# Moving the start of TensorE's SBUF tiles to multiples of 128 bytes in a hybrid decoder layer

## The chip, the cores and the metric

The kernel runs on one core of one Trainium2 chip. The metric is the device time of one execution in microseconds; each run gives one such time, and the median of three runs stands for the kernel.

## What is computed

One decoder layer on x of shape (1, 1024, 1024), float32. The reference, cut to its frame:

```python
def hybrid_layer(x, ...):
    h = rms_norm(x, norm1_g)
    z = h @ w_in                                  # 1024 x 2304
    ...                                           # pool | short conv | conformer conv | differential attention
    mix = jnp.concatenate([y_pool, y_sconv, y_conf, y_attn], axis=-1)
    x = x + mix @ w_out                           # 1024 x 1024
    h2 = rms_norm(x, norm2_g)
    x = x + (jax.nn.silu(h2 @ w_gate) * (h2 @ w_up)) @ w_down   # 1024 x 2816, 2816 x 1024
    return x
```

## The kernel before, in words

**The products.** Every large product is made to nearly full float32 precision of three matmuls in the type float32r: each operand is split into a rounded part (hi) and the rest (lo), and `mm3` (L133) adds hi·hi, hi·lo and lo·hi in PSUM. The first argument of a matmul is the stationary operand (`lhsT`, 128 columns, loaded before it), the second the moving one (`rhs`, up to 512 columns, streamed through). `mms` (L579) is the same three as a generator, so that they can be put between other work.

**The weights.** `wsplit` (L120) brings 128x1024 of a weight by DMA into a staging tile `st` (pool `stp`), casts it into `whi` (ACT, L116) and takes the rest into `wlo` (POOL, L130). Those two lie in pool `wp`, or in tiles of the tags `dw`, `pt0` and `pt1` in other pools.

**The stages.** They follow one another on TensorE, with overlap at the seams:

- Input projections into channels (`chunk_mm`, L222): the moving operand is `hT` (the normalized, transposed x, four tiles `hT00` to `hT11`), the stationary one `whi` or `wlo`. First with 256 columns (192 matmuls) while x is normalized, then with 512 (480). Beside them VectorE makes the convolutions (`conv_taps`, L292, its steps at L300) and GpSimd the pooling sums (`winsum`, L382).
- Projections of k, q and v (`proj_tok`, L449): the weight moves (256 columns), `hT` is stationary (576 matmuls).
- Attention in 16 units (`unit`, L633), between whose steps the output projection is put (`gen_partial`, L584, and `out_attn`, L718; its matmuls stand at L580 to L582, the weight moves with 512 columns, the tiles `sp`, `mh`, `ml` are stationary). `gen_partial` has 288 of them, `out_attn` 96.
- Gate and up (`gu_mm`, L785, and `gu_items`, L821): `h2` (tiles `h2a`, `h2b`, `h2c`, `h2lo`, `h2hi`) moves with 512 columns, the weight is stationary. There are 22 column tiles, 2 matrices, 2 halves of the sequence, 8 contraction tiles and 3 products: 2112 matmuls, into the PSUM tiles `pg` and `pu`.
- Down (`down`, L884): the weight moves with 512 columns, the activation tiles `a` are stationary; 11 groups of 96, 1056 matmuls into `pd`. In the first ten groups the weight is in the tag `dw`, in the last in `wp`.

The scheduler that orders each engine's work is the tile framework's (`schedule_with_timeline_sim`), with `tc.issue_after` at some places.

**Where a tile lies.** SBUF is 128 partitions of bytes; a tile begins at one byte address in all of them. Pools with `side="left"` are laid from low addresses upward behind a descriptor scratch of 16,384 bytes, pools with `side="right"` from the top (229,344) downward; a tile's size is rounded up to 32 bytes. Pool `sm` (small tiles) takes 5,056 bytes, 39.5 times 128, so that everything on the left behind it begins 64 bytes past a multiple of 128. The top is 96 bytes past one, and so is every large tile on the right. In the built program the operands of the large projections begin so many bytes past a multiple of 128:

| matmuls | columns | moving operand | stationary operand |
|---|---|---|---|
| projections into channels | 256, 512 | `hT`: 96 | `wp`: 0 |
| k, q, v | 256 | `wp`: 0 | `hT`: 96 |
| output projection | 512 | `wp`: 0 | `sp`, `mh`, `ml`: 64 |
| gate, up: 1968 | 512 | `h2`: 64 | `wp`: 0 |
| gate, up: 144, at the seam to attention | 512 | `h2`: 64 | `pt0`, `pt1`: 96 |
| down, first ten groups (960) | 512 | `dw`: 64 | `a`: 64 |
| down, last group (96) | 512 | `wp`: 0 | `a`: 64 |

A slice within a tile begins a multiple of 512 bytes further on, so that its offset is its tile's. In the text below such a pair is written (moving, stationary), (64, 0) for gate and up.

Of the kernel before, what the change touches and what calls it, by code (L numbers as in the profile page):

```python
# [11 lines left out]
F = mybir.dt.float32  # L12
# [7 lines left out]
P = 128  # L20
# [46 lines left out]
def tile_hybrid(ctx, tc, x, norm1_g, w_in, pool_w, pool_scale, sconv_w, conf_w, conf_b, ln_g, ln_b,  # L67
                q_g, k_g, lq1, lk1, lq2, lk2, subln_g, w_out, norm2_g, w_gate, w_up, w_down,
                rel_bias, onehot, maskrow, cntinv, out):
    nc = tc.nc  # L70
    V, A, G, T = nc.vector, nc.scalar, nc.gpsimd, nc.tensor
# [11 lines left out]
    def pool(name, bufs=1, side="left", **kw):  # L83
        return tc.tile_pool(name=name, bufs=bufs, side=side, reuse_waits="tile", **kw)
# [2 lines left out]
    stp = ctx.enter_context(pool("stp", 2))  # L87
    wp = ctx.enter_context(pool("wp", 6))
    sm = ctx.enter_context(pool("sm"))
    dram = ctx.enter_context(tc.tile_pool(name="dram", bufs=1, space=DRAM))  # L90
    m8 = ctx.enter_context(pool("m8", 3))
    spp = ctx.enter_context(pool("spp", 4))
# [12 lines left out]
    make_identity(nc, ident)  # L105
    mhalf = const.tile([P, 16], F, name="mhalf")
    G.memset(mhalf, -0.5)

    def col(name, src, n, pl=const):
        t = pl.tile([P, n], F, name=name)  # L110
        dma(out=t, in_=src.rearrange("o (c p) -> p (o c)", p=P))
        return t
# [846 lines left out]
```

## Time and profile before

| | |
|---|---|
| runs | 1191.39, 1189.75, 1190.41 us |
| median | 1190.41 us |
| the profiled execution: span from the first to the last instruction | 1189.3 us |
| TensorE matmul busy | 1143.7 us (96%) |
| VectorE, GpSimd, ScalarE busy | 570.3, 388.2, 338.6 us |
| bytes moved by DMA | 62.50 MB, 53 GB/s on the mean |

The profile gives no time of the profiled execution beyond its span; the median of the runs is 1.1 us longer than this span, which is the start and the end of the program. A matmul's duration in the profile (0.39 us for 512 columns) overlaps with its neighbours; what a matmul costs in a stream is the distance from its start to the next one's, and that is read from the timeline as the first and the last start of a stream and the number of matmuls between them.

### The profile page before, as it was taken

What the parts mean: (1) busy time and instruction counts of PE and PEld (TensorE: products, weight loads), DVE (VectorE), ACT (ScalarE), POOL (GpSimd) and SP (SyncE); (2) the same over time, 40 slices, a digit from 0 to 9 for tenths busy, and PEclk for the clock granted to TensorE, in tenths of its full rate; (3) what the DMA queues carried; (4) which work ended last, traced back from release to release, by engine and by line L of the source; (5) the groups of instructions that cost most, each with busy time, mean ns of one, the idle gap of its engine ahead of it and who ended that gap; (6) DMA issues with size and microseconds to landing.
All of it is one profiled execution on the core that took longest, in us unless ns stands there. A gap on an engine that the chain in (4) does not pass through costs nothing.

```text
span 1189.3 us, 13724 instructions
## 1 busy us (share of the span) xinstructions
PE 1143.7 (96%) x5563; PEld 944.9 (79%) x5563; DVE 570.3 (48%) x916; ACT 338.6 (28%) x614; POOL 388.2 (33%) x260
## 2 busy tenths in 40 slices
PE   7999399999989999999999999999999999999998
PEld 7877279997778768888888888888888888888887
DVE  5698984648999875314232322414132322314134
ACT  5411012546776765310212112020212112020200
POOL 5239224655677532320312221130312122130300
PEclk8999599999999999999999999999999999999999
DMA  8121111111121110311211111120211111120103
GB/s 214 53 62 36 36 35 37 37 37 36 36 81 36 45 54 19 107 53 36 71 36 54 53 36 54 36 60 30 72 36 53 53 41 49 36 71 19 53 1 141
DMA packets 85678, 62.50 MB, mean 53 GB/s; under 512 B 15560, under 2 KB 76528, under 8 KB 85616
## 3 DMA queue, kind: packets, MB, share of 16 engines
q1 hardware_dynamic: 85616, 61.64, 17.2%
q8 instruction: 43, 0.70, 0.2%
q14 instruction: 19, 0.16, 0.0%
HBM read 57.43 MB, written 4.20 MB: 52 GB/s over the span
## 4 chain that ended last, share of the span: by engine, by line
PE 83%; DVE 8%; issue 3%; ACT 2%; DMA 2%; POOL 1%; SPq 1%; ACTq 0%; POOLq 0%
PE pd L135 7%; PE pd L136 7%; PE pd L134 7%; PE pg L136 7%; PE pu L135 7%; PE pg L134 7%; PE pg L135 7%; PE pu L136 7%; PE pu L134 7%; PE mm L134 4%; PE mm L135 4%; PE mm L136 4%; DVE mixC L300 2%; PE fm L580 1%; PE fm L582 1%
## 5 line engine op out<-in xcount | busy, mean ns | idle before, releaser
L130 POOL TENSOR_TENSOR wlo<-st,whi 128x1024 fp32r<-128x1024 f32 (+1 forms) x92 | 238.3, 2597 | 631.9 <-ACT whi L116 611.4
L116 ACT CAST whi<-st 128x1024 fp32r<-128x1024 f32 x90 | 94.5, 1051 | 461.4 <-PE pd L135 207.3
L795 DVE TENSOR_TENSOR aa<-sg,pu 128x512 f32<-128x512 f32 x44 | 30.3, 688 | 338.6 <-PE pu L136 337.8
L894 DVE TENSOR_TENSOR x<-x,pd 128x512 f32<-128x512 f32 x176 | 120.1, 687 | 135.2 <-PE pd L136 135.1
L136 PE MATMUL pd<-whi,a 128*128 128x512 f32 x352 | 137.3, 390 | 0.0
L135 PE MATMUL pd<-wlo,a 128*128 128x512 f32 x352 | 137.3, 390 | 0.0
L134 PE MATMUL pd<-whi,a 128*128 128x512 f32 x352 | 137.2, 390 | 0.0
L135 PE MATMUL pu<-h2lo,whi 128*128 128x512 f32 x256 | 101.4, 396 | 0.0
L135 PE MATMUL pg<-h2lo,whi 128*128 128x512 f32 x256 | 101.3, 396 | 0.0
L300 DVE SCALAR_TENSOR_TENSOR mixC<-u,cw,mixC 128x1023 f32<-128x1023 f32 (+29 forms) x60 | 91.1, 1548 | 0.8
L135 PE MATMUL mm<-hT,whi 128*128 128x512 f32 (+1 forms) x224 | 82.8, 374 | 1.3 <-DVE hT L196 1.3
L134 PE MATMUL mm<-hT,whi 128*128 128x512 f32 (+1 forms) x224 | 80.9, 376 | 2.8 <-DVE t L428 1.6
L136 PE MATMUL mm<-hT,wlo 128*128 128x512 f32 (+1 forms) x224 | 82.3, 371 | 0.0
L135 PEld LDWEIGHTS pd<-wlo,a 128*128 128x128 f32 x352 | 66.1, 188 | 14.3
L134 PEld LDWEIGHTS pd<-whi,a 128*128 128x128 f32 x352 | 66.2, 188 | 14.0
L136 PEld LDWEIGHTS pd<-whi,a 128*128 128x128 f32 x352 | 66.1, 188 | 13.9
L798 DVE TENSOR_TENSOR a<-aa,a 128x512 fp32r<-128x512 f32 x44 | 63.7, 1447 | 25.2 <-ACT a L797 25.2
L134 PE MATMUL pg<-h2hi,whi 128*128 128x512 f32 x176 | 69.8, 396 | 0.0
L136 PE MATMUL pg<-h2hi,wlo 128*128 128x512 f32 x176 | 69.7, 396 | 0.0
L134 PE MATMUL pu<-h2hi,whi 128*128 128x512 f32 x176 | 69.7, 396 | 0.0
L136 PE MATMUL pu<-h2hi,wlo 128*128 128x512 f32 x176 | 69.7, 396 | 0.0
L797 ACT CAST a<-aa 128x512 fp32r<-128x512 f32 x44 | 27.2, 617 | 110.4 <-DVE aa L795 110.4
(266 smaller groups left out, 2333.9 us busy)
## 6 DMA issues: line engine op xcount, KB each, us to landing
st<-in_w_gate_dram SPq DMA_DIRECT2D x22, 512.0 KB, 3.7
st<-in_w_up_dram SPq DMA_DIRECT2D x22, 512.0 KB, 3.7
st<-in_w_down_dram SPq DMA_DIRECT2D x22, 512.0 KB, 3.4
st<-in_w_in_dram SPq DMA_DIRECT2D x18, 512.0 KB, 3.7
xt<-in_x_dram SPq DMA_DIRECT2D x8, 512.0 KB, 7.8
st<-in_w_out_dram SPq DMA_DIRECT2D x8, 512.0 KB, 3.5
xr<-in_x_dram SPq DMA_DIRECT2D x16, 256.0 KB, 2.6
out_dram<-x SPq DMA_DIRECT2D x7, 512.0 KB, 2.6
```

What stands on the lines that cost most here:

```text
L116: A.copy(dst, src)
L130: G.tensor_tensor(lo[:, nv:], st[:, nv:], hi[:, nv:].bitcast(F), op=ALU.subtract)
L134: T.matmul(ps, lhsT=L[0], rhs=Rr[0], start=first, stop=False)
L135: T.matmul(ps, lhsT=L[0], rhs=Rr[1], start=False, stop=False)
L136: return T.matmul(ps, lhsT=L[1], rhs=Rr[0], start=False, stop=last)
L300: V.scalar_tensor_tensor(acc[:, s:], u[:, :S - s], w[:, j:j + 1], acc[:, s:], op0=ALU.mult, op1=ALU.add)
L580: yield lambda: T.matmul(ps, lhsT=L[0], rhs=Rr[0], start=first, stop=False)
L582: yield lambda: T.matmul(ps, lhsT=L[1], rhs=Rr[0], start=False, stop=last)
L795: V.tensor_tensor(aa, sg, pu, op=ALU.mult)
L797: A.copy(a[0][:, j, sl], aa)
L798: V.tensor_tensor(a[1][:, j, sl], aa, a[0][:, j, sl].bitcast(F), op=ALU.subtract)
L894: V.tensor_tensor(x1[t][:, sl], x1[t][:, sl], ps, op=ALU.add)
```

## The change

Two tiles are added that nothing reads. `padl` (64 bytes) stands at the start of pool `sm`, and `padr` (96 bytes) is the first thing on the right side; each gets a memset on GpSimd. The descriptor scratch is halved to 8,192 bytes, since with both pads the left and the right side would no longer fit beside each other.

```diff
     stp = ctx.enter_context(pool("stp", 2))
     wp = ctx.enter_context(pool("wp", 6))
     sm = ctx.enter_context(pool("sm"))
+    padl = sm.tile([P, 16], F, name="padl")
+    padr = ctx.enter_context(pool("padr", side="right")).tile([P, 24], F, name="padr")
...
     G.memset(mhalf, -0.5)
+    G.memset(padl, 0.0)
+    G.memset(padr, 0.0)
...
-    nc = _bacc.Bacc("TRN2", target_bir_lowering=False, num_devices=1)
+    nc = _bacc.Bacc("TRN2", target_bir_lowering=False, num_devices=1, dynamic_dma_scratch_size=8192)
```

In the built program of the change all operands of the table above begin at a multiple of 128 bytes, every pair is (0, 0). Tiles that TensorE reads in smaller steps move too: `pt`, `KT`, `QT`, `VV`, `kst` to 0, the normalized x before its transposes (`xn`) from 32 to 96, `sa` and `pu` of the pooling part from 32 to 96 (`pu1` from 96 to 32). The staging tiles `st` stay at 0.

The instructions of TensorE, VectorE, ScalarE and SyncE are the same, in the same order. Only GpSimd's differ, at its start, before (the tile `ident` is the identity for transposes, `rn` the first norm of x):

```order
masks.py:197 MEMSET ident 128x128
L107 MEMSET mhalf 128x16
L363 MEMSET anti 128x128
masks.py:199 ISA
masks.py:199 AFFINE_SELECT ident<-ident 128x128
L367 MEMSET bd 128x256
L364 AFFINE_SELECT anti<-anti 128x128
L169 TENSOR_SCALAR rn<-ssf 128x1
```

and with the change (its lines are 2 to 4 further on):

```order
masks.py:197 MEMSET ident 128x128
L109 MEMSET mhalf 128x16
L110 MEMSET padl 128x16
L111 MEMSET padr 128x24
masks.py:199 ISA
masks.py:199 AFFINE_SELECT ident<-ident 128x128
L367 MEMSET anti 128x128
L371 MEMSET bd 128x256
L368 AFFINE_SELECT anti<-anti 128x128
L173 TENSOR_SCALAR rn<-ssf 128x1
```

Two small memsets have come ahead of the making of `ident`, and the memset of `anti` has moved behind it.

## Rows read from the trace of the kernel before

**Rows 1.** The page: busy time by engine, and the chain's shares by engine.
```profile
PE 1143.7 (96%) x5563; PEld 944.9 (79%) x5563; DVE 570.3 (48%) x916; ACT 338.6 (28%) x614; POOL 388.2 (33%) x260
PE 83%; DVE 8%; issue 3%; ACT 2%; DMA 2%; POOL 1%; SPq 1%; ACTq 0%; POOLq 0%
```
**Rows 2.** Busy time by stage: us, each engine's busy us, clock, DMA share, GB/s.
```profile
53.00:141.00 88.00, 68.33 (x275) 51.22 (x274) 83.11 (x66) 13.61 (x18) 51.10 (x20) 0.89 0.19 54
141.00:190.00 49.00, 48.81 (x202) 38.71 (x203) 39.43 (x36) 5.78 (x8) 9.93 (x5) 0.96 0.11 33
190.00:269.00 79.00, 79.00 (x684) 79.00 (x683) 38.95 (x78) 37.15 (x74) 47.28 (x36) 1.00 0.11 34
269.00:440.00 171.00, 158.75 (x876) 130.02 (x876) 148.92 (x375) 119.37 (x273) 102.91 (x102) 0.99 0.16 50
440.00:541.00 101.00, 100.39 (x453) 80.48 (x452) 35.02 (x52) 35.74 (x58) 27.87 (x15) 1.00 0.20 58
541.00:1163.00 622.00, 622.00 (x2693) 506.39 (x2691) 184.91 (x233) 97.52 (x127) 129.42 (x54) 1.00 0.15 44
1163.00:1189.30 26.30, 22.38 (x98) 18.05 (x96) 11.70 (x17) 0.00 (x0) 0.00 (x0) 1.00 0.40 160
```
**Rows 3.** Timeline of TensorE, gate and up, (64, 0): start us, us, instruction.
```profile
1041.24 0.39 PE L134 MATMUL pu<-h2a,whi 128*128 128x512 f32 x1
...
1074.84 0.39 PE L134 MATMUL pd<-whi,a 128*128 128x512 f32 x1
```
**Rows 4.** Timeline of TensorE, down, its tenth group, (64, 64).
```profile
1141.45 0.39 PE L134 MATMUL pd<-whi,a 128*128 128x512 f32 x1
...
1163.00 0.39 PE L136 MATMUL pd<-whi,a 128*128 128x512 f32 x1
```
**Rows 5.** Timeline of TensorE, down, its last group, (0, 64).
```profile
1163.22 0.40 PE L134 MATMUL pd<-whi,a 128*128 128x512 f32 x1
...
1184.98 0.40 PE L136 MATMUL pd<-whi,a 128*128 128x512 f32 x1
```
**Rows 6.** Timeline of TensorE, up with its weight in `pt1` and `pt0`, (64, 96).
```profile
483.36 0.40 PE L135 MATMUL pu<-h2lo,whi 128*128 128x512 f32 x1
...
496.89 0.39 PE L136 MATMUL pu<-h2hi,wlo 128*128 128x512 f32 x1
```
**Rows 7.** Timeline of TensorE, projections into channels, (96, 0).
```profile
160.01 0.39 PE L135 MATMUL mm<-hT,whi 128*128 128x512 f32 x1
...
176.33 0.40 PE L136 MATMUL mm<-hT,wlo 128*128 128x512 f32 x1
```
**Rows 8.** Timeline of TensorE, projections of k, q, v, 256 columns, (0, 96).
```profile
249.62 0.28 PE L136 MATMUL mm<-whi,hT 128*128 128x256 f32 x1
...
257.91 0.28 PE L136 MATMUL mm<-whi,hT 128*128 128x256 f32 x1
```
**Rows 9.** Timeline of TensorE, projections into channels at half clock, (96, 0).
```profile
142.20 0.63 PE L136 MATMUL mm<-hT,wlo 128*128 128x512 f32 x1
...
143.91 0.63 PE L134 MATMUL mm<-hT,whi 128*128 128x512 f32 x1
```
**Rows 10.** Busy time of TensorE in that stretch: us, busy, clock, DMA share, GB/s.
```profile
141.19:144.60 3.41, 3.41 (x8) 0.50 0.00 0
```
**Rows 11.** Groups of TensorE instructions by line and form: busy us, mean ns, idle before.
```profile
L135 PE MATMUL mm<-hT,whi 128*128 128x512 f32 x160 | 64.0, 400 | 0.0
L135 PE MATMUL mm<-wlo,hT 128*128 128x256 f32 x192 | 54.1, 282 | 0.0
```
**Rows 12.** Waits of TensorE: us in total, times, longest us.
```profile
PE mm L417 <- DVE t L428: 15.2, 1, 15.2
```
**Rows 13.** The page's DMA queues: packets, MB, share of the 16 engines.
```profile
q1 hardware_dynamic: 85616, 61.64, 17.2%
```
**Rows 14.** Timeline of GpSimd at the start.
```profile
0.86 0.11 POOL L107 MEMSET mhalf<- 128x16 f32 x1
...
5.38 0.31 POOL L169 TENSOR_SCALAR rn<-ssf 128x1 f32<-128x1 f32 x1 [3.43 <-ACT xn L166]
```

## The prediction

> **What bounds the kernel now.** First the page: TensorE is busy in 96% of the span and makes 83% of the chain that ended last [rows 1]. Then the stages [rows 2]: from 440 us on TensorE is busy in 100.4 of 101, 622 of 622 and 22.4 of 26.3 us, and in 190 to 269 us in all of 79, while VectorE and GpSimd have far less to do there. In those stages what each matmul takes off passes straight to the end. In 269 to 440 us (attention) TensorE has 158.8 us and VectorE 148.9 of 171: the chain alternates. In 53 to 141 us VectorE is busy in 83.1 of 88 us, and TensorE ends that stage in a wait of 15.2 us for it [rows 2, 12]: what TensorE gains before 141 us only lengthens that wait.
>
> Third, the cost of one matmul in a stream, read as the first and the last start and the count between. A clock at full speed should need 512 columns' time and no more. At half clock that is so: four steps take 1.71 us, 427.5 ns each, with the clock at 0.50 [rows 9, 10], one column in each cycle of 1.2 GHz. Half of it, 213.3 ns, is what 2.4 GHz would give. At full clock every stream is slower than that, and by how much goes with where the two operands begin:
>
> - (64, 0), gate and up: 144 matmuls in 33.60 us, 233.3 ns [rows 3]
> - (64, 96), up at the seam: 58 in 13.53 us, 233.3 ns [rows 6]
> - (96, 0), channels: 70 in 16.32 us, 233.1 ns [rows 7]
> - (0, 64), last down group: 95 in 21.76 us, 229.0 ns [rows 5]
> - (64, 64), other down groups: 95 in 21.55 us, 226.8 ns [rows 4]
> - (0, 96), 256 columns: 71 in 8.29 us, 116.8 ns, against 106.7 [rows 8]
>
> So 13 to 20 ns of each matmul, 6 to 9%, are lost at full clock alone, which points to the reading of operands and not to the array. The least is lost where both operands begin at the same offset. No row shows (0, 0) for such a matmul; it has to be bounded.
>
> **The price of (0, 0).** Take the loss over 213.3 ns as a sum: a part b that always stands, A if the moving operand begins off a multiple of 128, B if the stationary one does, C if the two offsets differ. The four kinds of 512 columns give b+A+B = 13.5, b+A+C = 20.0, b+A+B+C = 20.0 and b+B+C = 15.7. Hence C = 6.5, B = 0, A = 4.3 and b = 9.2: (0, 0) would take **222.5 ns**. The ends: no loss at all, 213.3 ns; and from the same rows taken as if each operand had its own price (moving from 64 to 0 costs 229.0 - 226.8 = 2.2, stationary from 64 to 0 costs 233.3 - 226.8 = 6.5), 226.8 + 8.7 = 235.5 ns. I take 222.5, since it alone fits all four kinds. For 256 columns I take half of what 512 save from a moving operand at 0: (229.0 - 222.5) / 2 = 3.25 ns.
>
> **The change part by part.** The instructions of four engines are the same in the same order, so only prices and waits move.
>
> - Gate and up: 2112 x (233.3 - 222.5) = 22.8 us, in stages where TensorE never waits.
> - Down, ten groups: 10 x 96 = 960 matmuls; 960 x 4.3 = 4.1 us. The last group: 96 x 6.5 = 0.6 us.
> - Channels: of 480 (3 x 160) [rows 11] 192 come after 141 us, and 8 of these run at half clock [rows 10], where nothing is lost: 184 x 10.8 = 2.0 us. VectorE has 39.4 of 49 us there, so TensorE sets the time. The 288 before, and the 192 with 256 columns, I cost at nothing, since the 15.2 us wait covers them; if all came through they would bring 3.1 us and about 1, and if GpSimd and VectorE collide otherwise when TensorE's results come 2 us earlier, as much may be lost.
> - k, q, v: 576 (3 x 192) [rows 11] x 3.25 = 1.9 us.
> - Output projection: 384, of which 24 already run between gate and up. 360 x 6.5 = 2.3 us, of which I count half, 1.2 us, as the chain in attention is VectorE's as often; the ends are 0 and 2.3.
> - The two memsets: the small one there takes 0.11 us, and the first norm on GpSimd comes 4.5 us later, after a wait of 3.43 us for ScalarE [rows 14]. Nothing, or 0.2 us at the worst, if the making of `ident` is late.
> - The scratch: 61.64 of 62.50 MB are moved by the hardware queue of SyncE [rows 13], whose order is unchanged. Nothing.
>
> In the big stages nothing is late next: in 541 to 1163 us GpSimd is busy in 129, VectorE in 185 of 622 us and DMA in 15% [rows 2]. The sum is 32.6 us: 1189.3 becomes 1156.7 us of span, and with the 1.1 us by which the median is longer, 1190.4 becomes **1157.8 us**. With (0, 0) anywhere from 219 to 226 ns the same sum gives 46.0 to 19.2 us, 1144 to 1171 us: that is this case's own range.
>
> [...]
>
> **The rivals.**
>
> 1. *The loss is gone altogether.* 226.8 is 17/16 of 213.3: 2048 bytes that begin amid a piece of 128 touch 17 pieces and not 16. If whole pieces are what is fetched, and different phases of the two operands make the rest, (0, 0) takes 213.3 to 219 ns. In the middle, 216: 36.5 (gate, up) + 10.4 + 1.2 (down) + 3.2 (channels) + 3.7 (k, q, v) + 2.3 (output) = 57.3 us, **1133 us**; at 213.3, 67.7 us and 1123 us. For it: the 17/16 is exact, and at half clock nothing is lost. Against it: (0, 64) has its moving operand in place and still loses 15.7 ns. [...]
> 2. *Only the difference counts.* (0, 0) is as (64, 64), 226.8: 13.7 + 0.2 + 1.2 + 0.6 + 0.4 = 16.1 us, **1174 us**. For it: the three kinds with unequal offsets are the slow ones. Against it: (64, 0) and (0, 64) differ by 4.3 ns, so that a place of its own counts too.
> 3. *Only the moving operand counts*, (0, 0) is as (0, 64), 229.0: gate and up give 9.1 us, channels 0.8, down loses 2.1: **1183 us**. [...]
> 4. *Starts don't matter.* The difference between rows 3 and 4 would come from how gate, up and down are built (24 matmuls into one PSUM tile against 6), and the change moves nothing: **1190 us**. Against it: rows 6 and 7 with quite other tiles agree with rows 3 to 0.2 ns, and rows 5 and 4, both down, differ by 2.2. [...]
> 5. *Slower: each operand has its own price, and 64 is the good place for both.* This is the other end above, 235.5 ns: gate and up lose 4.6 us, down 8.4 + 0.6, the rest 3.5: **1207 us**. It decides from 231 ns for (0, 0) upward, the mean of today's prices weighted by the counts above. For it: taking the stationary operand from 64 to 0 does cost 6.5 ns in the rows, and the moving one 2.2. Against it: it needs (64, 96) to be as slow as (64, 0) by chance, where unequal offsets explain both.
>
> That the change doesn't do what it says is out: in the built program every pair is (0, 0).
>
> **How the numbers follow.** My case 0.38, rival 1 0.27, rival 2 0.15, rival 3 0.05, rival 4 0.03, rival 5 0.12. The forecast is the first. The range 1126 to 1178 us holds the first three cases, 0.80, from near the whole loss of rival 1 to somewhat over rival 2's time, for gains in attention that don't come through. A measurement of this kernel tells 0.2%, 2.4 us, from no change: the first four make faster, 0.85; rival 4 is the same, 0.03; rival 5 slower, 0.12.
>
> **What would show it.** In the changed profile the streams of rows 3 and 4 should have one and the same distance, near 222 ns; 216 is rival 1, 227 rival 2, 233 or more for down rival 5. Rows 8 should come to about 113.5 ns, the wait of 15.2 us should grow by 2 to 4 us, and 541 to 1163 us should shrink by some 23 us with TensorE still always busy. I am wrong if the streams of gate, up and down keep different distances, or if TensorE begins to wait in that stage.

## The result, and the profile after

The change takes 1178.26 us (median, 1177.47 to 1178.78) beside 1190.15 us for the kernel before on the same chip: a ratio of 0.9897, 95% interval 0.9883 to 0.9911. It is faster by 11.9 us, where 32.4 were forecast, and lies just outside the range that was given. The profiled execution has a span of 1175.7 us, 13.6 less than before.

The page reads as before, a little shorter [rows 1]:

```profile
PE 1129.4 (96%) x5563; PEld 943.7 (80%) x5563; DVE 571.3 (49%) x916; ACT 339.0 (29%) x614; POOL 388.3 (33%) x262
PE 83%; DVE 8%; issue 3%; ACT 2%; POOL 2%; DMA 1%; SPq 1%; ACTq 0%; POOLq 0%
```

The answer lies in the distances between matmuls. Five streams of the changed kernel in TensorE's timeline (start us, us, instruction), each by its first and last row: gate and up, down, channels, k, q, v, and the seam (up with its weight in `pt1` and `pt0`), which answer to [rows 3], [rows 4, 5], [rows 7], [rows 8] and [rows 6]:

```profile
1022.72 0.39 PE L138 MATMUL pg<-h2b,whi 128*128 128x512 f32 x1
...
1062.61 0.39 PE L140 MATMUL pu<-h2hi,wlo 128*128 128x512 f32 x1
...
1128.12 0.39 PE L138 MATMUL pd<-whi,a 128*128 128x512 f32 x1
...
1171.41 0.39 PE L140 MATMUL pd<-whi,a 128*128 128x512 f32 x1
...
159.28 0.39 PE L139 MATMUL mm<-hT,whi 128*128 128x512 f32 x1
...
175.54 0.39 PE L140 MATMUL mm<-hT,wlo 128*128 128x512 f32 x1
...
189.08 0.28 PE L139 MATMUL mm<-wlo,hT 128*128 128x256 f32 x1
...
194.60 0.28 PE L140 MATMUL mm<-whi,hT 128*128 128x256 f32 x1
...
483.34 0.40 PE L139 MATMUL pu<-h2lo,whi 128*128 128x512 f32 x1
...
496.83 0.40 PE L140 MATMUL pu<-h2hi,wlo 128*128 128x512 f32 x1
```

| stream | matmuls between | ns each, now | before | forecast |
|---|---|---|---|---|
| gate, up | 176 | 226.7 | 233.3 | 222.5 |
| seam | 58 | 232.6 | 233.3 | 222.5 |
| down, last two groups together | 191 | 226.7 | 226.8 and 229.0 | 222.5 |
| channels, 512 columns | 70 | 232.3 | 233.1 | 222.5 |
| k, q, v, 256 columns | 46 | 120.0 | 116.8 | 113.5 |

So gate and up fell to what down had, but for their 144 matmuls at the seam, which hardly fell; of down only the last group fell; channels hardly fell, and k, q, v rose. The stream shown of k, q, v is one of the slower ones: over the 536 distances in that stage that hold no gap (all under 160 ns) the mean is 118.9 ns, against 116.8 before, and from its first to its last matmul the stage takes 80.23 us in place of 79.14. TensorE still never waits in the long stage, and the wait in the channels for VectorE is 15.6 us in place of 15.2 [rows 12], in these rows of the stages (TensorE's busy time alone, clock, DMA share, GB/s) and of the waits:

```profile
190.00:269.00 79.00, 79.00 (x675) 1.00 0.11 34
540.60:1171.60 631.00, 631.00 (x2785) 1.00 0.16 49
```
```profile
PE mm L421 <- DVE t L432: 15.6, 1, 15.6
```

From the first gate matmul to the last down matmul the two traces have 744.43 us (440.55 to 1184.98) and 730.68 us (440.73 to 1171.41). These 13.75 us are the gain of the span. Ahead of that stage the change is 0.2 us later: it reaches the first k, q, v matmul 0.8 us earlier, k, q, v take 1.1 us more, and attention 0.1 us less.

The median fell by less than the span. A run takes 1.8 us more than its own span (1177.47 and 1175.7 us in the profiled execution of the change), not the 1.1 us that the median of before suggested. So the profiled execution of before, at about 1191.1 us, was one of the slower ones of its kernel, and that of the change the fastest of its four.

### The profile page after: what moved, and what is told of

The parts are those of the page before. It is cut to its first block, busy times and chain, and to the rows that moved or that the text cites. A ratio compares the mean times of both kernels' runs of the same rounds, so it can differ in the third digit from the quotient of the medians.

```text
span 1175.7 us, 13726 instructions
## 1 busy us (share of the span) xinstructions
PE 1129.4 (96%) x5563; PEld 943.7 (80%) x5563; DVE 571.3 (49%) x916; ACT 339.0 (29%) x614; POOL 388.3 (33%) x262
## 4 chain that ended last, share of the span: by engine, by line
PE 83%; DVE 8%; issue 3%; ACT 2%; POOL 2%; DMA 1%; SPq 1%; ACTq 0%; POOLq 0%
PE pd L138 7%; PE pd L139 7%; PE pd L140 7%; PE pg L140 6%; PE pu L140 6%; PE pu L139 6%; PE pu L138 6%; PE pg L139 6%; PE pg L138 6%; PE mm L138 4%; PE mm L139 4%; PE mm L140 4%; DVE mixC L304 2%; PE fm L586 1%; PE fm L584 1%
## 5 line engine op out<-in xcount | busy, mean ns | idle before, releaser
L138 PEld LDWEIGHTS pd<-whi,a 128*128 128x128 f32 x352 | 66.1, 188 | 13.6
```

The lines of the kernel that those rows point to most:

```text
L138: T.matmul(ps, lhsT=L[0], rhs=Rr[0], start=first, stop=False)
```

## Experiments

**The theory after the result.** Down at (64, 64) before, and gate, up and down at (0, 0) now, take the same 226.7 to 226.8 ns, so it seems to be the difference that counts and not the place. But the streams with a tile of the right side (`hT`, `pt0`, `pt1`) did not get there. In the built program `hT` begins at 163,712, an odd multiple of 128, while the tiles on the left begin at multiples of 256. Theory D: with d for how far the stationary operand begins behind the moving one, modulo 256 bytes, a matmul's distance is a function of d. In the change, channels, k, q, v and the seam have d = 128, the other large products 0; in the kernel before gate and up had 64 (and 32 at the seam), channels 32, k, q, v 224, the last down group and the output projection 192. The main rival, E, is the change's own idea: a start at a multiple of 128 is good for each operand.

**One pad at a time.** `left_only` leaves out `padr`:

```diff
-    padr = ctx.enter_context(pool("padr", side="right")).tile([P, 24], F, name="padr")
...
-    G.memset(padr, 0.0)
```

> Only the left pad (and the halved scratch); the right side begins as in the kernel before. Theory D (what counts is how far the stationary operand begins behind the moving one, modulo 256 bytes or less): gate, up and down at 226.8 ns as with both pads; k, q, v back from 119.9 to 116.8 ns, since hT is again 224 bytes past a multiple of 256 against the weight; channels back to 233.3 ns. So about 1.5 us faster than the change, near 1176.7 us. Rival E (each operand gains by its own start at a multiple of 128): the right pad is worth something, so this run is slower than the change, over 1178.3 us.

Measured: 1176.77 us (1176.54 to 1177.20), ratio to the kernel before 0.9883, 0.9868 to 0.9898. k, q, v in its timeline, 47 matmuls in 5.49 us, 116.8 ns:

```profile
190.27 0.28 PE L136 MATMUL mm<-whi,hT 128*128 128x256 f32 x1
...
195.76 0.28 PE L138 MATMUL mm<-whi,hT 128*128 128x256 f32 x1
```

`right_only` leaves out `padl` in the same way.

> Only the right pad (and the halved scratch); the left side begins 64 bytes off again. Theory D: gate and up at 233.3, down at 226.8 and 229.0 in its last group, as before; k, q, v at 119.9, channels at 232.4; 1.5 us slower than the kernel before, near 1191.7 us. Rival E: some gain in channels and k, q, v, so 1 to 4 us faster than before.

Measured: 1191.60 us beside 1190.82, ratio 1.0008, 0.9999 to 1.0017. Both came out as D has it, and rival E falls, which wanted `left_only` slower than the change and `right_only` 1 to 4 us faster than before. What the right pad costs is small: `right_only` is 0.8 us over the kernel before, with 1 inside its interval, and `left_only` 1.5 us under the change, all its runs below all of the change's, though not measured beside them. The traces have it in the stage of k, q, v, 79.10 us in `left_only` and 80.23 in the change. So the left pad alone is worth at least the whole change. `right_only` has the halved scratch too, and its gate and up stay at 233.3 ns: the scratch has no part in their gain.

The seam, with its weights on the right and `h2` on the left, passes through four values of d in these kernels. The 58 matmuls of the table take 233.3 ns before (d = 32), 232.6 in the change (128), 233.4 in `left_only` (224) and 229.1 in `right_only` (192), where of all that the stream reads only the weight's start differs between the change and `left_only`.

**Where hT belongs.** The right pad is made larger:

```diff
-... .tile([P, 24], F, name="padr")
+... .tile([P, 56], F, name="padr")
```

> The right pad is 224 bytes in place of 96, so that hT begins at a multiple of 256 (256 past one of 512) as the tiles on the left do. Theory D with modulus 256: channels fall from 232.4 to 226.8 ns, k, q, v from 119.9 to about 113.4 (half of 226.8); 1.0 and 3.7 us, near 1173.5 us. Rival F (128 is the step that counts, and what hT still loses comes from its place or from the work beside it): no difference from the change, 1178.3 us. Rival G (modulus 512 or more): little or no difference here.

> The right pad is 480 bytes, so that hT begins at a multiple of 512. Theory D with modulus 256: the same as with 224 bytes, near 1173.5 us. Rival F: no difference from the change. Rival G: here, and only here, channels at 226.8 and k, q, v near 113.4 ns.

Measured: 1176.32 us (ratio 0.9880, 0.9866 to 0.9893) and 1176.66 us (0.9882, 0.9869 to 0.9896), all their runs below those of the change, by 1.6 to 1.9 us in the median, though not measured beside it, and not to be told from one another: the modulus is 256 or less. Channels with 224 bytes, 70 in 15.88 us, now take 226.9 ns:

```profile
159.15 0.40 PE L139 MATMUL mm<-hT,whi 128*128 128x512 f32 x1
...
175.03 0.39 PE L140 MATMUL mm<-hT,wlo 128*128 128x512 f32 x1
```

D was right there, and at the seam (226.7 ns, d = 0). It was wrong for 256 columns: k, q, v have 120.0 ns (47 in 5.64 us) and 119.7 on the mean of the stage, not 113.4. For them d = 224 with 116.8 is better than d = 0, which is why this run is not the forecast 1173.5 us.

**All multiples of 128 taken away.** `all64` puts every large tile 64 bytes past a multiple of 256:

```diff
+    padc = const.tile([P, 16], F, name="padc")
+    G.memset(padc, 0.0)
...
-... .tile([P, 24], F, name="padr")
+... .tile([P, 40], F, name="padr")
```

> Every large tile begins 64 bytes past a multiple of 256, those that TensorE reads and the staging tiles alike: a pad of 64 bytes ahead of the staging pool, the one in the pool of small tiles kept, the right pad 160 bytes. Theory D: no start is a multiple of 128, but all differences are 0, so 226.7 ns everywhere, 120.0 ns in k, q, v, and the time of the right pad of 224 bytes, 1176.3 us, or 2 us faster than the change. Rival E: 64 past a multiple is a bad start, so slower than the change, toward 1190 us.

Measured: 1176.86 us (1176.58 to 1176.98), ratio 0.9883, 0.9869 to 0.9898. No large tile begins at a multiple of 128, gate and up are at 226.7 ns, and the kernel is as fast as with all at 256.

**The function of d.** In two sweeps the weight tiles lie in slots of 4352 bytes and begin `off` bytes into them, by another number in each group:

```diff
-        hi = (wpool or wp).tile([P, 1024], R, name="whi", tag=tag)
...
+        wide, o = (1024, 0) if tag[:2] == "pt" else (1088, off // 4)
+        hi = (wpool or wp).tile([P, wide], R, name="whi", tag=tag)[:, o:o + 1024]
...
```

> As the kernel with a right pad of 224 bytes, but each group of gate and up, of down, and each of k, q, v has its weight tiles begin so many bytes further on within larger slots (all else at a multiple of 256). Gate and up by group 1 to 10: 0, 16, 32, 64, 96, 128, 160, 192, 224, 240. Down by group 0 to 9 the same ten. k, q, v: 32, 64, 96. Writing d for the start of the stationary operand behind the moving one, modulo 256, d is that number in gate and up, and 256 less it in down and k, q, v. Theory D (the matmul's distance is a function of d alone): 0: 226.8; 32 and 64: 233.3; 128: 232.4; 192: 229.0; 224: 233.3 ns, in gate and up and in down alike where d is the same; k (d 224) 116.7 ns. 16, 96, 160 and 240 have no row yet, between 226 and 234. Rival H (the place of each operand by itself counts): down, whose moving operand is shifted, differs from gate and up at the same d. Rival I (the kind of product counts, starts don't): all groups of gate and up alike, all of down alike.

> As the first sweep with other shifts. Gate and up by group 1 to 10: 4, 8, 48, 80, 112, 144, 176, 208, 248, 256; down by group 0 to 9 the same ten; k, q, v: 224, 16, 128. Theory D: 256 is as 0, 226.8 ns; 4, 8 and 248 (252 to 248 and 8 in down) tell whether equal starts are one sharp point or the middle of a valley: sharp gives 233 ns already at 4, a valley of 64 bytes or more gives 227 to 229. k (d 32) 118.7, v (d 128) 119.7 ns. Rival H and rival I as in the first sweep.

Each sweep was executed once, with its profile. Gate and up, ns by d, each over 176 matmuls (191 at 4, 286 at 0):

| d | 0 | 4 | 8 | 16 | 32 | 48 | 64 | 80 | 96 | 112 |
|---|---|---|---|---|---|---|---|---|---|---|
| ns | 226.8 | 232.4 | 230.7 | 226.7 | 233.4 | 233.4 | 233.3 | 232.0 | 234.3 | 233.3 |
| **d** | **128** | **144** | **160** | **176** | **192** | **208** | **224** | **240** | **248** | **256** |
| ns | 232.4 | 233.3 | 233.4 | 230.1 | 228.9 | 231.9 | 233.4 | 228.3 | 233.3 | 226.7 |

Three of these streams, of the first sweep, by their first and last rows: d = 16, 192 and 224.

```profile
563.85 0.39 PE L142 MATMUL pg<-h2b,whi 128*128 128x512 f32 x1
...
603.74 0.39 PE L144 MATMUL pu<-h2hi,wlo 128*128 128x512 f32 x1
...
965.40 0.39 PE L142 MATMUL pg<-h2b,whi 128*128 128x512 f32 x1
...
1005.68 0.40 PE L144 MATMUL pu<-h2hi,wlo 128*128 128x512 f32 x1
...
1031.81 0.40 PE L142 MATMUL pg<-h2b,whi 128*128 128x512 f32 x1
...
1072.88 0.39 PE L144 MATMUL pu<-h2hi,wlo 128*128 128x512 f32 x1
```

They are 226.7, 228.9 and 233.4 ns apart. All that the rows of before showed is in the table: 233.3 at 32 and 64, 229.0 at 192, 226.8 at 0. Rival I falls. Equal starts are neither one sharp point nor the middle of a smooth valley: 232.4 at 4, 230.7 at 8, 226.7 at 16, 233.4 at 32. No d goes under 226.7.

In down, where the moving operand is shifted, the same d gives the same time within 0.3 ns at d = 0, 32, 64, 96, 128, 160 and 224 (means of the four windows of 24 matmuls in each group). At 192 it doesn't: two of the four windows take 229.6 ns, as in the table, and two 233. The second and the third of them:

```profile
744.89 0.40 PE L142 MATMUL pd<-whi,a 128*128 128x512 f32 x1
...
750.17 0.39 PE L144 MATMUL pd<-whi,a 128*128 128x512 f32 x1
...
751.57 0.40 PE L142 MATMUL pd<-whi,a 128*128 128x512 f32 x1
...
756.94 0.40 PE L144 MATMUL pd<-whi,a 128*128 128x512 f32 x1
```

These windows have the same tiles and the same d. In q of the same sweep, d = 192 too, one stream of 25 takes 113.3 ns each and the next one, of 35, 117.8:

```profile
232.95 0.28 PE L143 MATMUL mm<-wlo,hT 128*128 128x256 f32 x1
...
235.79 0.28 PE L144 MATMUL mm<-whi,hT 128*128 128x256 f32 x1
...
236.47 0.28 PE L143 MATMUL mm<-wlo,hT 128*128 128x256 f32 x1
...
240.59 0.28 PE L142 MATMUL mm<-whi,hT 128*128 128x256 f32 x1
```

So one d can hold two steady distances, and which of them a stream takes is not shown. Shifts of the moving operand that are no multiple of 32 part from the table more widely: d = 16 by moving it gives 236.3 ns (95 in 22.45 us). So with 512 columns and shifts of 32 bytes d settles the distance, except at 192. Theory D in its full form, d alone for all, doesn't hold, and below 32 bytes rival H has its share.

**k, q, v by themselves.** `best` keeps d = 0 and begins the weights of k, q, v 32 bytes further on (`off=32` in those slots).

> All operands at multiples of 256 as with the right pad of 224 bytes, but the weights of k, q and v begin 32 bytes further on in slots of 4352 bytes (d 224). Theory D: matmuls of 512 columns at 226.7, k, q, v at 116.7 ns against 120.0; 576 x 3.3 = 1.9 us off 1176.3, near 1174.4 us. Rival E (starts at whole multiples are what helps): slower than with the right pad of 224 bytes.

Measured: 1176.29 us (1174.23 to 1176.46), no difference from 1176.32. The stream is at 116.7 ns as expected, and from its first matmul to its last the stage is 79.06 us in place of 80.63; the profile of `best` reaches that stage 0.9 us later. The forecast of 1174.4 us did not come as a time of the kernel (one of four runs has 1174.23); the gain shows in the stage alone.

**Where the last 13 ns come from.** At equal starts 226.7 ns stand 13.3 ns over 213.3. The latter is an estimate from the half clock [rows 9]: a longer stream of the kernel before at a clock of 0.50, with 256 columns, has 25 distances in 5.33 us, 213.2 ns each or 1.2 columns in a ns. At twice the clock that would be 106.6 ns for 256 columns and 213.2 for 512. Its first and last row, and below them TensorE's busy time there (us, busy, clock, DMA share, GB/s):

```profile
16.11 0.41 PE L136 MATMUL mm<-hT,wlo 128*128 128x256 f32 x1
...
21.44 0.41 PE L135 MATMUL mm<-hT,whi 128*128 128x256 f32 x1
```
```profile
16.10:21.40 5.30, 5.30 (x26) 0.50 0.84 84
```

`onecol` leaves all starts equal and takes away reading:

```diff
...
+            if g in (3, 4, 7, 8):
+                R_ = tuple(r[:, 0:1].broadcast_to([P, 512]) for r in R_)
+            if g in (5, 6, 7, 8):
+                L = tuple(l[:, 0:1].broadcast_to([P, P]) for l in L)
...
```

> As with the right pad of 224 bytes (all d 0); in gate and up of groups 3 and 4 the moving operand is its first column 512 times over (step 0), in 5 and 6 the stationary operand is its first column 128 times over, in 7 and 8 both: the products of these groups are not the layer's. It asks where the 13.3 ns come from that stay at equal starts. If they are the reading of the moving operand (2048 bytes), groups 3, 4, 7, 8 fall from 226.7 to 213 to 216 ns; if they are the reading of the stationary one, groups 5 to 8 do; if they come from neither read (the exchange of weights in the array, for instance), all stay at 226.7 ns.

Group 3 (the moving operand is one column) and group 5 (the stationary one is), first and last row of 176 matmuls each:

```profile
630.25 0.38 PE L138 MATMUL pg<-h2b,whi 128*128 128x512 f32 x1
...
668.24 0.38 PE L140 MATMUL pu<-h2hi,wlo 128*128 128x512 f32 x1
...
757.14 0.40 PE L138 MATMUL pg<-h2b,whi 128*128 128x512 f32 x1
...
797.82 0.39 PE L140 MATMUL pu<-h2hi,wlo 128*128 128x512 f32 x1
```

37.99 us are 215.9 ns, 40.68 us are 231.1 ns. Groups 7 and 8, with both at one column, take 215.8 ns. So 10.9 of the 13.3 ns go with the reading of the moving operand; the stationary one read at a single place makes it worse, not better, and only while the moving one is read along. What the last 2.5 ns over 213.3 are stays open.

`patterns` asks which reading:

```diff
+    def again(r, n):
+        return r[:, 0:n].unsqueeze(1).broadcast_to([P, 512 // n, n])
+    def mixed(r, n):
+        return r.rearrange("p (a b) -> p b a", a=n)
...
```

> As with the right pad of 224 bytes (all d 0), but in gate and up of groups 2 to 6 the moving operand is its first 256, 128, 64, 32 or 8 columns over and over until 512 are streamed; in group 7 all 512 columns alternately from the two halves, in group 8 first the even and then the odd ones, in group 9 in steps of 64 columns (256 bytes): the products of these groups are not the layer's. One column 512 times gave 215.8 ns against 226.7. If the 10.9 ns are one piece more to be fetched at the start of each matmul, 2 to 6 all fall short of 226.7 only when nothing new is fetched at all: 226.7 for 256 to 32 columns, and 7 to 9 at 226.7 or more. If they are meetings with the read of the weights at the same place modulo 256 bytes, 256, 128 and 64 columns (1024, 512 and 256 bytes, which pass every such place) stay at 226.7, 32 and 8 columns (128 and 32 bytes) fall toward 216, and group 9, which moves its place by 4 bytes only after 8 columns, falls or rises clearly.

The first 256, 128 and 64 columns over and over: 226.7 ns. 32 columns: 236.7. 8 columns: 216.6. The even ones and then the odd ones: 453. In steps of 64 columns: 487. And all 512 alternately from the two halves: 215.8. The granted clock is 1.00 in all of them, and 0.989 over the whole execution. Groups 2, 5, 7 and 8 (the even ones first) by their first and last rows (154, 164, 156 and 176 matmuls):

```profile
565.01 0.39 PE L140 MATMUL pg<-h2b,wlo 128*128 128x512 f32 x1
...
599.92 0.39 PE L138 MATMUL pu<-h2hi,whi 128*128 128x512 f32 x1
...
761.12 0.40 PE L140 MATMUL pg<-h2b,wlo 128*128 128x512 f32 x1
...
799.93 0.40 PE L139 MATMUL pu<-h2lo,whi 128*128 128x512 f32 x1
...
891.18 0.38 PE L139 MATMUL pg<-h2lo,whi 128*128 128x512 f32 x1
...
924.85 0.38 PE L139 MATMUL pu<-h2lo,whi 128*128 128x512 f32 x1
...
957.82 0.61 PE L138 MATMUL pg<-h2b,whi 128*128 128x512 f32 x1
...
1037.59 0.64 PE L140 MATMUL pu<-h2hi,wlo 128*128 128x512 f32 x1
```

Neither guess fits. One more piece at the start would leave 8 columns and the halves at 226.7; meetings at the same place modulo 256 would spare 32 columns. What is shown is only that the order in which the moving operand is read sets the loss, and that one order which reads everything has none of the 10.9 ns.

**A version that uses it.** `woven` streams the moving operands of gate, up and down alternately from their halves. PSUM then holds the columns in that order, and the instructions that read it put them back:

```diff
+    def weave(v):
+        return v.rearrange("p (a b) -> p b a", a=2)
+    def woven(v):
+        return v.rearrange("p (b a) -> p b a", a=2)
...
-            mm3(ps, (W[0][:, kt], W[1][:, kt]), h2rhs(h, kt), kt == 0, kt == 7)
+            mm3(ps, (W[0][:, kt], W[1][:, kt]), tuple(map(weave, h2rhs(h, kt))), kt == 0, kt == 7)
...
-        A.copy(a[0][:, j, sl], aa)
+        A.copy(weave(a[0][:, j, sl]), woven(aa))
...
-                V.tensor_tensor(x1[t][:, sl], x1[t][:, sl], ps, op=ALU.add)
+                V.tensor_tensor(weave(x1[t][:, sl]), weave(x1[t][:, sl]), woven(ps), op=ALU.add)
```

> On the right pad of 224 bytes: in gate, up and down each moving operand of 512 columns is streamed alternately from its two halves, columns 0, 256, 1, 257 and so on, as in the group that took 215.8 ns; the result stands in PSUM in that order and is put right by VectorE and ScalarE when they write it on, so that the layer is computed in full. If reading the moving operand straight through is what costs the 10.9 ns and the rest is unharmed: 215.8 ns in gate, up and down, 2112 + 1056 times 10.9 = 34.5 us off 1176.3, near 1142 us. If VectorE or ScalarE become slow on the strided writes, the matmuls show 215.8 ns but TensorE waits for PSUM, and the gain is smaller; if 215.8 ns came from something else in that group, no gain.

Measured: 1141.98 us (1141.60 to 1143.00), ratio 0.9595, 0.9582 to 0.9608. Gate and up, and down, by first and last rows (176 and 191 matmuls), 215.8 ns both:

```profile
931.98 0.38 PE L144 MATMUL pg<-h2b,whi 128*128 128x512 f32 x1
...
969.96 0.38 PE L146 MATMUL pu<-h2hi,wlo 128*128 128x512 f32 x1
...
1094.50 0.38 PE L144 MATMUL pd<-whi,a 128*128 128x512 f32 x1
...
1135.72 0.38 PE L146 MATMUL pd<-whi,a 128*128 128x512 f32 x1
```

The strided work costs the other engines: the addition to x1 takes 1092 ns in place of 686, as the page's group shows, and VectorE is busy in 57% of the span. It still waits for TensorE there, so that only the last addition reaches the end of the kernel: 1.06 us in place of 0.69.

```profile
L904 DVE TENSOR_TENSOR x<-x,pd 128x512 f32<-128x512 f32 x176 | 189.3, 1092 | 55.1 <-PE pd L146 55.1
```

`woven_kq` does the same with the weights of k and q (`proj_tok(C_K, use_k, wv=weave)`, and in `qk_norm` a copy out of PSUM that puts the columns back).

> As the kernel before it, and the weights of k and q (256 columns) are streamed from their two halves in turn too, 512 bytes apart in place of 1024. If that distance does as well: 108.3 ns in place of 120.0 in 384 matmuls, 4.5 us more off, near 1137 us. If only 1024 bytes do, no difference from the kernel before it, or a loss.

Measured: 1139.38 us (1138.58 to 1139.88), ratio 0.9571, 0.9558 to 0.9584, faster than `woven` by 2.6 us and by its whole spread. The stream took 111.6 ns (47 in 5.24 us), not 108.3, in the timeline:

```profile
189.15 0.27 PE L144 MATMUL mm<-whi,hT 128*128 128x256 f32 x1
...
194.39 0.28 PE L146 MATMUL mm<-whi,hT 128*128 128x256 f32 x1
```

384 x (120.0 - 111.6) is 3.2 us; the stage is 3.1 us shorter than in `woven` (77.56 and 80.62), and the median 2.6. Whether d still counts when an operand is streamed from its halves was not run.

## Why the prediction was wrong

- *What bounds the kernel* was right: TensorE is never idle in the long stage before or after, and 13.75 us of shorter matmuls there are the gain. Also right is that most of the loss lies in the reading of operands: with the moving operand read at one column only, 215.9 of the 226.7 ns are left, with as many matmuls of as many columns.
- *The price of (0, 0)* is the step that failed. The sum b + A + B + C put A = 4.3 ns on a moving operand that begins off a multiple of 128, because (64, 0) and (0, 64) differ by that much. They differ since their d are 64 and 192, and the table of d is not the same on both sides of 128: 233.3 and 228.9. With A gone, b is 13.3 to 13.5, not 9.2, and (0, 0) is 226.7, not 222.5. Four kinds of stream fitted four unknowns, so the fit could not speak against its own form. The 213.3 ns under the sum are an estimate from the half clock (1.2 columns in a ns there, twice as many at the full one); no run shows a stream of 512 columns below 215.8 ns.
- *The step of 128 bytes* was wrong beside it, and was taken from the change. Rows 3 and 5 held the pair that tells 128 from 256: their difference is 64 modulo 128 in both, and they lie 4.3 ns apart. The prediction read that as a price of the moving operand's place.
- *Gate and up*: forecast 22.8 us; (2112 - 144) x (233.3 - 226.7) is 13.0, and the seam with d = 128 gives 144 x 0.8 ns = 0.1. *Down*: forecast 4.7; only the last group gained, 96 x 2.3 ns = 0.2.
- *Channels*: forecast 2.0 us; 184 x 0.8 ns = 0.1, since `hT` went to an odd multiple of 128 and d to 128. *k, q, v*: forecast a gain of 1.9 us; a loss of 576 x 2.1 ns = 1.2 came on the mean distances, 1.1 in the stage, from d = 224 to 128.
- *Output projection*: forecast 1.2 us; from the last k, q, v matmul to the first of gate the two traces have 171.61 and 171.53 us, 0.1 less. The kernels with other pads have 170.9 to 171.7 there, so that a gain of this size can't be told.
- *Channels before 141 us, memsets, scratch at nothing*: right, as far as the sums show. The wait was to grow by 2 to 4 us and grew by 0.4, since these matmuls hardly became shorter.
- *Rival 2* (only the difference counts) named the mechanism, with 0.15, and its sign, 227 ns in gate, up and down alike, is the one that came. Its 1174 us miss the measured time by what channels, k, q, v, the seam and the output projection did; what was held against it, rows 3 against 5, falls with the step of 256. *Rival 1* falls by the same streams: with every start at a multiple of 256 they still take 226.7 ns, so that 17/16 of 213.3 is not the price of a start amid a piece of 128. No operand read straight through came into its 213.3 to 219 ns; 215.8 came in `woven`, by another order of reading. *Rival 3* falls by the sweep: the stationary start alone moves the distance between 226.7 and 234.3 ns. Rows 3 and 4, with one and the same moving start and 6.5 ns apart (233.3 and 226.8), stood against it already. *Rival 4* falls with gate, up and down now alike, *rival 5* with them and with `all64`.

## What to carry to other kernels

Read a stream's cost as the distance between starts and compare it with half of what such a matmul takes at a granted clock of 0.50 (here about 213 ns for 512 columns, from 427.5); where it is longer, as here by 6 to 9% (226.8 to 233.3 ns), the order and the starts of what TensorE reads are worth a sweep, and one run with another offset in each group measures ten of them. Here equal starts modulo 256 bytes of the two operands brought 3% of a matmul of 512 columns (233.3 to 226.7 ns), at multiples of 256 as at 64 bytes past them, and streaming such an operand alternately from its halves another 5% (226.7 to 215.8). With 256 columns equal starts were not the best: 119.7 ns, against 116.8 at d = 224. A pad chosen by a round number on one side can undo there a part of what another brings: `padr` lengthened k, q, v by 1.1 us.

## What was not expected of the hardware

- A float32r matmul of 512 columns takes 226.7 ns when its moving operand is read straight through and 215.8 ns when it is read alternately from two places 1024 bytes apart; with 256 columns and 512 bytes, 120.0 and 111.6. The order from the halves is the fastest measured that reads the whole operand; the even columns followed by the odd ones take 453 ns, steps of 64 columns 487.
- The distance depends on the two operands' starts modulo 256 bytes (d = 256 has 226.7 ns as d = 0 has), down to single words: d = 4 costs 5.7 ns over d = 0 (232.4 and 226.7), d = 16 nothing (226.7) when the stationary operand is the one that is shifted. At d = 192 one and the same start gave two steady distances, 229.6 and 233 ns, or 113.3 and 117.8 with 256 columns.
- A stationary operand read 128 times at one place makes a matmul slower, 231.1 against 226.7 ns. Why, and why the halves in turn have none of the 10.9 ns, stays open.
